# Where the tiles of a one-core encoder block begin in SBUF: small tiles rounded up to 64 bytes

## The chip, the core and the metric

The kernel runs on one core of a Trainium2 chip. The metric is the device time of one execution in microseconds (us), and the median of three executions counts. TensorE (PE in the profile) does the matrix products, VectorE (DVE) and ScalarE (ACT) work on vectors, GpSimd (POOL) and SyncE (SP) mostly issue transfers. SBUF is the on-chip memory from which PE reads both of its operands: the stationary one (the weights, by a LDWEIGHTS instruction, "PEld") and the moving one, which streams through the array in a MATMUL.

## The reference

One layer of an encoder for 256 tokens of width 2048, all in float32:

```
h   = rms_norm(x, norm_g[0])
q, k, v, g, lr, u_f, u_h, u_s = split(h @ w_in)
mix = concat(gla(q, k, v, g, lr), rms_norm(fnet(u_f)),
             rms_norm(hyena(u_h)), rms_norm(shortconv(u_s)))
x   = x + mix @ w_out
x   = x + cross_attention(rms_norm(x, norm_g[1]), rms_norm(mem, mem_norm_g)) # w_xq, w_xkv, w_xo
x   = x + (silu(h3 @ w_gate) * (h3 @ w_up)) @ w_down   # h3 = rms_norm(x, norm_g[2])
return rms_norm(x, final_norm_g)
```

Nearly all of the work is the seven matrices: 4032 blocks of 128x128 weights, each against 256 tokens.

## The kernel before

**Two halves of each number.** To multiply in float32 with fast matmuls, each operand is held as a high part and the rest. A slot of activations is a tile of 128 partitions by 512 columns (2048 bytes in a partition): columns 0 to 255 hold the high part of 256 tokens, columns 256 to 511 the rest. Weights arrive as slabs of 16 blocks (`raw`, 8192 bytes in a partition) by DMA from SP's queue at L79. For each half of a slab ScalarE writes the high part `wh` (L89) and VectorE the rest `wl` (L90). `raw` and `wh`, `wl` rotate through three buffers each, with a fourth pair of `wh`, `wl` until the end of the attention's output product.

**Three ways to multiply by a block.** The method `mm` has two of them. The wide form (L269 and L270) loads `wh` and streams the whole slot, 512 columns, then loads `wl` and streams its first 256 columns. The narrow form (L266, L267 and L270) does three matmuls of 256 columns; it is used in part of the mixers' `w_in` and for the last output tile of `w_down`. The third is `gemm_rows` (L321 to L323): here the activations are stationary, and `wh`, `wl` are the moving operands, 512 columns in each of six matmuls for four blocks. It makes the values of the attention and of the gated linear attention.

**Stages.** In order: keys and values of the memory (`w_xkv`), the mixers (`w_in`), `w_out`, queries and attention (`w_xq`, `w_xo`), the gate and up products (`w_gate_up`), and `w_down`. Between blocks a planner (`Background.poll`) lets generators issue the vector work of earlier results. The order on each engine is fixed when the program is built.

**Slots.** The moving slots are `act0` to `act23` in every stage. In `w_xo`, four of the sixteen are `oex0` to `oex3`. In `w_down`, eight of the 44 are `act` and 36 are `f0` to `f35`. Attention itself streams `kt` (against the stationary `q`, L637 and L638) and `pt` (against `vh`, `vl`, L664 and L665).

**Where the tiles lie.** The pools hand out SBUF in the order in which the tiles are asked for, and each takes its bytes in a partition rounded up to a multiple of 32. The slots `act` and the residuals `res` come first and begin at multiples of 64. Then comes `vec`, 150 columns of float32 or 600 bytes, which takes 608; all that is asked for after it begins 32 bytes past a multiple of 64, until other small tiles shift it back. From the address table of the built program, the start of each tile as a remainder:

| tile | mod 64, before | mod 256, before | mod 64, after | mod 256, after |
|---|---|---|---|---|
| `act`, `res` | 0 | 128 | 0 | 128 |
| `ones`, `ident`, `acc` | 32 | 224 | 0 | 0 |
| `tmp`, `dg` | 32 | 96 | 0 | 192 |
| `raw`, `wh`, `wl` | 32 | 224 | 0 | 0 |
| `f`, `oex`, `pt` | 32 | 224 | 0 | 0 |
| `k2`, `tab`, `gw` and most tiles of the mixers | 32 | 96 | 0 | 128 |
| `kt`, `q`, `vh`, `vl`, `mr` | 0 | 0 | 0 | 64 |

The lines that the change touches are L51 (`NV`, the columns of `vec`), L224 (the columns of scalars of a reciprocal root, `rc` and `krc`), L351 (`warm`), L409 (`sums`), L553 (`qs`) and L645 (the scalars of a softmax).

Of the kernel before, what the change touches and what calls it, by code (L numbers as in the profile page):

```python
# [13 lines left out]
F32 = mybir.dt.float32  # L14
# [8 lines left out]
P = 128  # L23
# [24 lines left out]
V_SCW = 133  # L48
V_B1, V_B2, V_FR = 145, 146, 147
V_NT = 148  # L50
NV = 150  # L51

TWO_PI_1 = 6.28125
TWO_PI_2 = float(np.float32(2 * math.pi - 6.28125))
# [95 lines left out]
class Block:  # L150
# [68 lines left out]
    def rstd_cols(self, p, n, keep=None):  # L219

        nc = self.nc
        m = p.shape[1]
        self.bg.dve(0, 8)
        c = keep.tile([P, 24], F32, name=f"krc{next(self.kept)}") if keep else self.rp.tile([P, 24], F32, name="rc", tag="rc")  # L224
        y, v, a = (c[:, 8 * i:8 * i + m] for i in range(3))
        nc.vector.tensor_scalar(out=v, in0=p, scalar1=1.0 / n, scalar2=EPS, op0=ALU.mult, op1=ALU.add)

        nc.vector.tensor_scalar(out=a.bitcast(U32), in0=v.bitcast(U32), scalar1=1, scalar2=None, op0=ALU.logical_shift_right)
        nc.vector.tensor_scalar(out=y.bitcast(I32), in0=a.bitcast(I32), scalar1=-1.0, scalar2=float(0x5f3759df),
                                op0=ALU.mult, op1=ALU.add)  # L230
        for _ in range(3):
            self.stt(a, y, -0.5, y, ALU.mult, ALU.mult)
            self.tt(a, a, v, ALU.mult)
            self.stt(y, a, 1.5, y, ALU.add, ALU.mult)
        return y
# [95 lines left out]
    def run(self):  # L331
        nc, cp = self.nc, self.cp
        st = self.st
        self.act = [cp.tile([P, 512], F32R, name=f"act{i}") for i in range(24)]
        self.res = [cp.tile([P, 4, R], F32, name=f"res{i}") for i in range(4)]
        self.resk = lambda i: self.res[i // 4][:, i % 4, :]
        self.vec = cp.tile([P, NV], F32, name="vec")
        self.ones = cp.tile([P, P], F32, name="ones")
        self.ident = cp.tile([P, P], F32, name="ident")
        self.acc = cp.tile([P, R], F32, name="acc")  # L340

        self.kd = nc.dram_tensor("keys", (P, 16 * R), F32, kind="Internal").ap()
        self.vd = nc.dram_tensor("values", (P, 8 * 512), F32, kind="Internal").ap()
        nc.scalar.dma_start(self.vec, self.t["vecs"])
        def load(src, k, n):
            nc.sync.dma_start(self.res[k // 4][:, k % 4:k % 4 + n, :].rearrange("p k r -> p (k r)"),
                              self.t[src][:, k * R:(k + n) * R])

        self.load_x = lambda k, n: load("xT", k, n)

        warm = cp.tile([P, 1], F32, name="warm")  # L351
        nc.vector.memset(warm, 1.0)
        nc.scalar.copy(warm, warm)
        load("memT", 0, 1)
        st.after = [lambda: None, lambda: None]
        st.after += [lambda a=a: load("memT", *a) for a in ((1, 1), (2, 1), (3, 1), (4, 1), (5, 1), (6, 2), (8, 2), (10, 2), (12, 2), (14, 2))]
        nc.vector.memset(self.ones, 1.0)
        make_identity(nc, self.ident)
        with self.tc.tile_pool(name="wx", bufs=1) as st.extra:
            self.mixers()  # L360
            self.attention()
        self.mlp()
# [5 lines left out]
    def mixers(self):  # L368
# [37 lines left out]
            nc.vector.tensor_reduce(out=c[:, 0:2], in_=c[:, 2:10].rearrange("p (r k) -> p r k", k=4), axis=AX.X, op=ALU.add)  # L406

        def prepare(mid):
            c = [mid.tile([P, 10], F32, name=f"sums{i}") for i in range(2)]  # L409
            yield 20  # L410
            yield from squares("mem", c[0])
            self.rcm = self.rstd_cols(c[0][:, 0:2], D, self.cp)
            yield
            self.rsm = self.rstd_end(self.rcm, 0, self.cp)
            self.bg.add(hy.filters())
            nc.sync.dma_start(gl.lrw, self.t["lrw"])
            yield from squares("x", c[1])
            col = self.rstd_cols(c[1][:, 0:2], D)
            yield
            self.rsx = self.rstd_end(col, 0, mid)  # L420
# [126 lines left out]
    def attention(self):  # L547
        tc, nc, act, st = self.tc, self.nc, self.act, self.st
        with tc.tile_pool(name="atp", bufs=1) as atp, tc.tile_pool(name="kp", bufs=1) as kp, \
                tc.tile_pool(name="mp", bufs=5) as mp:  # L550
            oex = [atp.tile([P, 512], F32R, name=f"oex{i}") for i in range(4)]
            pt = [atp.tile([P, 512], F32R, name=f"pt{i}") for i in range(2)]
            qs = atp.tile([P, 2], F32, name="qs")  # L553
            o = act[0:8] + oex + act[8:12]
            slot = lambda name, n: kp.tile([P, 512], F32R, name=name, tag=name, bufs=n)
            kv = [([], [], []) for _ in range(4)]

            def ev_q(q, p):
                q.append(slot("q", 8))
                self.split(q[-1], self.merge(p))  # L560

            def scales():

                col = self.rstd_begin([[self.acc]], D)
                nc.vector.tensor_scalar(out=qs, in0=col, scalar1=512 ** -0.5, scalar2=None, op0=ALU.mult)
                yield

            heads = []

            def load_kv():  # L570

                todo = [(hd, what, i) for hd in range(4) for what in range(2) for i in range(4)]
                parts = []

                def fetch():
                    if len(parts) < len(todo):
                        hd, what, i = todo[len(parts)]
                        m = mp.tile([P, R], F32, name="mr", tag="mr")
                        o = (4 * hd + i) * R
                        nc.gpsimd.dma_start(m, (self.vd if what else self.kd)[:, o:o + R])  # L580
                        parts.append(m)

                for _ in range(5):
                    fetch()
                yield 4
                for n, (hd, what, i) in enumerate(todo):
                    while hd > len(heads) + 1:
                        yield
                    if what == 0:
                        kv[hd][0].append(slot("kt", 8))  # L590
                        self.split(kv[hd][0][-1], parts[n])
                    else:
                        if i % 2 == 0:
                            kv[hd][1].append(slot("vh", 4))
                            kv[hd][2].append(slot("vl", 4))
                        c = slice(i % 2 * R, i % 2 * R + R)
                        self.split2(kv[hd][1][-1][:, c], kv[hd][2][-1][:, c], parts[n])
                    fetch()
                    yield 1.0

            def scores(hd, q):
                while len(kv[hd][2]) < 2:
                    yield
                yield
                yield from self.head(q, *kv[hd], pt, o[4 * hd:4 * hd + 4], qs)
                heads.append(hd)

            lp = [list(range(8)), list(range(8, 16))]
            self.bg.add(scales())
            self.bg.add(load_kv())  # L610
            gens = []
            for hd in range(4):
                q = []
                if hd > 1:
                    self.bg.drain(gens[hd - 2], True)
                self.gemm("w_xq", [(4 * hd + i) * P for i in range(4)], self.h2, lambda i, p: ev_q(q, p), first=(4, lp),
                          before=lambda n: n and hd == 0 and self.bg.drain(self.late))
                gens.append(self.bg.add(scores(hd, q)))
            h3 = self.h3 = act[12:24] + act[0:4]

            def ev_o(i, p):
                self.residual(i, p, V_NG + 32 + i, h3[i] if i < 12 else None)
                if i == 12:
                    st.extra = None

            self.gemm("w_xo", [i * P for i in range(16)], o,
                      ev_o,
                      first=(4, [list(range(12)), list(range(12, 16))]), before=lambda n: n == 1 and self.bg.drain())
            self.bg.add(self.rest(h3, 12, V_NG + 32))

    def head(self, q, kt, vh, vl, pt, o, qs):
# [10 lines left out]
        for r in range(2):  # L642
            s = self.merge(ps[r])
            self.tt(s, s, self.rsm, ALU.mult)
            c = self.rp.tile([P, 4], F32, name="rc", tag="sm")  # L645
            nc.vector.tensor_reduce(out=c[:, 0:1], in_=s, axis=AX.X, op=ALU.max)
            self.stt(c[:, 1:2], c[:, 0:1], -1.0, qs[:, r:r + 1], ALU.mult, ALU.mult)
            nc.scalar.activation(s, s, AF.Exp, scale=qs[:, r:r + 1], bias=c[:, 1:2], accum_out=c[:, 2:3])
# [591 lines left out]
```

## Time and profile before

| | us |
|---|---|
| median of three runs | 1525.95 (1525.63 to 1526.79) |
| the profiled execution | 1526.68 |
| its span, first to last instruction | 1524.6 |
| PE busy in the span | 1502.2 |
| DVE busy | 995.5 |
| ACT busy | 787.3 |
| mean granted clock of PE | 0.995 |

The time of the profiled execution is 2.1 us more than its span. A matmul's duration in the profile (394 ns for 512 columns) includes the time in which the next one already streams, since matmuls are pipelined. What a block costs is read from the starts: the time from the start of a matmul to the start of the next.

### The profile page before, as it was taken

Reading aid. Unit: us, or ns where it says so; the run is one execution under the profiler, and the core shown is the slowest. Engines: PE = TensorE matmul, PEld = TensorE weight load, DVE = VectorE, ACT = ScalarE, POOL = GpSimd, SP = SyncE. Lnnn points to the kernel's source line nnn. Section 1 sums busy time; section 2 is a strip of 40 time slices with the busy share of each in tenths; the row PEclk is TensorE's granted clock in tenths of the full one; section 3 lists DMA queues with packets and bytes.
Section 4 is the critical chain, followed back from the end, with each engine's and each line's share of the span. In section 5 each row is a group of like instructions: output and inputs, shape, how many; then the busy total and the mean of one; then the engine's idle time right before and its main releaser. Section 6 shows DMA issues by size and latency. Waiting matters only on the chain.

```text
span 1524.6 us, 22257 instructions
## 1 busy us (share of the span) xinstructions
PE 1502.2 (99%) x8788; PEld 1311.2 (86%) x8788; DVE 995.5 (65%) x1532; ACT 787.3 (52%) x1238; POOL 40.0 (3%) x76
## 2 busy tenths in 40 slices
PE   8999999999999999999999999999999999999996
PEld 7887788889999788888888888888888888888885
DVE  6676668678667766867766666666666664555454
ACT  6664555557445655656554444444444444444442
POOL 0100100000002000100000000000000000000000
PEclk9999999999999999999999999999999999999998
DMA  9965554354346555544545555555555555555552
GB/s 353 343 239 190 198 193 166 139 195 159 139 167 241 195 190 182 177 149 166 194 166 193 189 185 185 189 192 194 193 193 186 186 186 190 192 192 180 183 191 83
DMA packets 48808, 290.53 MB, mean 191 GB/s; under 512 B 6173, under 2 KB 7486, under 8 KB 17088
## 3 DMA queue, kind: packets, MB, share of 16 engines
q1 hardware_dynamic: 44912, 279.59, 51.5%
q0 software_dynamic: 3072, 8.39, 1.6%
q8 instruction: 69, 1.13, 0.3%
q10 hardware_dynamic: 720, 1.13, 0.2%
q14 instruction: 35, 0.29, 0.0%
HBM read 282.80 MB, written 6.29 MB: 190 GB/s over the span
## 4 chain that ended last, share of the span: by engine, by line
PE 96%; DVE 1%; DMA 1%; issue 1%; ACT 0%; SPq 0%; POOL 0%; DVEq 0%; POOLq 0%; ACTq 0%
PE pg L269 49%; PE pg L270 28%; PE pg L266 3%; PE pg L267 3%; PE pg L321 3%; PE pg L323 2%; PE pg L322 2%; PE pm L269 1%; PE pm L796 1%; DMA mr<-values 1%; PE pm L664 1%; PE pm L270 0%; PE pm L637 0%; DMA raw<-in_W 0%; DVE wl L90 0%
## 5 line engine op out<-in xcount | busy, mean ns | idle before, releaser
L269 PE MATMUL pg<-act,wh 128*128 128x512 f32 x2680 | 939.7, 394 | 8.3 <-DVE act L182 4.5
L90 DVE TENSOR_TENSOR wl<-raw,wh 128x1024 fp32r<-128x1024 f32 (+1 forms) x507 | 617.0, 1218 | 425.9 <-ACT wh L89 423.6
L270 PE MATMUL pg<-act,wl 128*128 128x256 f32 x3008 | 842.5, 281 | 0.0
L89 ACT CAST wh<-raw 128x1024 fp32r<-128x1024 f32 (+1 forms) x507 | 529.5, 1046 | 589.5 <-PE pg L269 333.4
L269 PEld LDWEIGHTS pg<-act,wh 128*128 128x128 f32 x2680 | 504.7, 188 | 120.7 <-ACT wh L89 4.5
L270 PEld LDWEIGHTS pg<-act,wl 128*128 128x128 f32 x3008 | 566.9, 189 | 2.6 <-issue 2.0
L269 PE MATMUL pg<-f,wh 128*128 128x512 f32 x540 | 191.3, 398 | 0.0
L270 PE MATMUL pg<-f,wl 128*128 128x256 f32 x576 | 161.8, 281 | 0.0
L269 PEld LDWEIGHTS pg<-f,wh 128*128 128x128 f32 x540 | 101.5, 188 | 25.2
L270 PEld LDWEIGHTS pg<-f,wl 128*128 128x128 f32 x576 | 108.8, 189 | 0.0
L266 PE MATMUL pg<-act,wh 128*128 128x256 f32 x328 | 94.8, 289 | 0.0
L267 PE MATMUL pg<-act,wh 128*128 128x256 f32 x328 | 92.1, 281 | 0.0
L178 DVE TENSOR_TENSOR tmp<-pg,tmp 128x256 f32<-128x256 f32 x183 | 76.2, 417 | 5.7 <-ACT tmp L276 5.0
L276 ACT COPY tmp<-pg 128x256 f32<-128x256 f32 x179 | 65.0, 364 | 14.6 <-PE pg L270 14.5
L321 PE MATMUL pg<-wh,act 128*128 128x512 f32 x160 | 66.4, 415 | 0.0
L323 PE MATMUL pg<-wh,act 128*128 128x512 f32 x160 | 63.3, 395 | 0.0
L322 PE MATMUL pg<-wl,act 128*128 128x512 f32 x160 | 62.9, 393 | 0.0
L266 PEld LDWEIGHTS pg<-act,wh 128*128 128x128 f32 x328 | 61.9, 189 | 0.7
L267 PEld LDWEIGHTS pg<-act,wh 128*128 128x128 f32 x328 | 61.9, 189 | 0.3
L178 DVE TENSOR_TENSOR tmp<-tmp,rs 128x256 f32<-128x256 f32 x88 | 37.3, 425 | 2.9
L321 PEld LDWEIGHTS pg<-wh,act 128*128 128x128 f32 x160 | 30.0, 188 | 10.4 <-issue 2.9
L322 PEld LDWEIGHTS pg<-wl,act 128*128 128x128 f32 x160 | 30.1, 188 | 7.5 <-issue 1.0
(233 smaller groups left out, 985.1 us busy)
## 6 DMA issues: line engine op xcount, KB each, us to landing
raw<-in_W SPq DMA_DIRECT2D x247, 1024.0 KB, 4.8
raw<-in_W SPq DMA_DIRECT2D x9, 512.0 KB, 7.3
res<-in_xT SPq DMA_DIRECT2D x8, 512.0 KB, 5.6
k<-in_mem SPq DMA_DIRECT2D x8, 256.0 KB, 9.0
k<-in_x SPq DMA_DIRECT2D x8, 256.0 KB, 8.2
keys<-tmp POOLq DMA_DIRECT2D x16, 128.0 KB, 5.7
values<-tmp POOLq DMA_DIRECT2D x16, 128.0 KB, 2.4
mr<-keys POOLq DMA_DIRECT2D x16, 128.0 KB, 3.5
```

The source lines that it names most:

```text
L89: nc.scalar.copy(wh[:, a:b], r[:, a:b])
L90: nc.vector.tensor_tensor(out=wl[:, a:b], in0=r[:, a:b], in1=wh[:, a:b].bitcast(F32), op=ALU.subtract)
L178: self.nc.vector.tensor_tensor(out=out, in0=a, in1=b, op=op)
L266: self.nc.tensor.matmul(p[:, 0:R], wh, slot[:, 0:R], start=start, stop=False)
L267: self.nc.tensor.matmul(p[:, 0:R], wh, slot[:, R:512], start=False, stop=False)
L269: self.nc.tensor.matmul(p[:, :], wh, slot[:, :], start=start, stop=False)
L270: self.nc.tensor.matmul(p[:, 0:R], wl, slot[:, 0:R], start=False, stop=stop)
L276: self.nc.scalar.copy(t, p[:, R:512])
L321: nc.tensor.matmul(ps[r][:, :], hi, wh, start=k == 0, stop=False)
L322: nc.tensor.matmul(ps[r][:, :], hi, wl, start=False, stop=False)
L323: nc.tensor.matmul(ps[r][:, :], lo, wh, start=False, stop=k == nk - 1)
L664: nc.tensor.matmul(p[:, :], vh[m][:, s], pt[m][:, :], start=m == 0, stop=False)
```

## The change

Six small tiles are made a multiple of 64 bytes: `vec` has 160 columns in place of 150 (640 bytes), the scalars of a reciprocal root 32 in place of 24 (128 bytes), the softmax's scalars 16 in place of 4, `sums` 16 in place of 10, and `warm` and `qs` take 16 columns, of which the first one and the first two are used. The host fills the ten new columns of `vec` with zeros. Every tile of 256 bytes or more then begins at a multiple of 64 (table above). The instructions of each engine and their order are the same in both programs, but for the DMA of `vec` (L344), which brings 128x160 numbers in place of 128x150.

```diff
-NV = 150
+NV = 160
...
-        c = keep.tile([P, 24], F32, name=f"krc{next(self.kept)}") if keep else self.rp.tile([P, 24], F32, name="rc", tag="rc")
+        c = keep.tile([P, 32], F32, name=f"krc{next(self.kept)}") if keep else self.rp.tile([P, 32], F32, name="rc", tag="rc")
...
-        warm = cp.tile([P, 1], F32, name="warm")
+        warm = cp.tile([P, 16], F32, name="warm")[:, 0:1]
...
-            c = [mid.tile([P, 10], F32, name=f"sums{i}") for i in range(2)]
+            c = [mid.tile([P, 16], F32, name=f"sums{i}") for i in range(2)]
...
-            qs = atp.tile([P, 2], F32, name="qs")
+            qs = atp.tile([P, 16], F32, name="qs")[:, 0:2]
...
-            c = self.rp.tile([P, 4], F32, name="rc", tag="sm")
+            c = self.rp.tile([P, 16], F32, name="rc", tag="sm")
```

## The prediction

> **What bounds the kernel now.** I read the page first, then the chain of waits, then the starts of the matmuls in the timeline.
>
> ```profile
> span 1524.6 us, 22257 instructions
> ...
> PE 1502.2 (99%) x8788; PEld 1311.2 (86%) x8788; DVE 995.5 (65%) x1532; ACT 787.3 (52%) x1238; POOL 40.0 (3%) x76
> ...
> PE 96%; DVE 1%; DMA 1%; issue 1%; ACT 0%; SPq 0%; POOL 0%; DVEq 0%; POOLq 0%; ACTq 0%
> ```
>
> PE sets the end: 96% of the chain is its matmuls. The program after has the same instructions in the same order, so the change can move the time only if an instruction's speed depends on where its tiles begin. The trace holds that comparison already, because some moving operands begin at a multiple of 64 bytes (`act`, `kt`) and others 32 past one (`f`, `oex`, `pt`, and `wh`, `wl` in `gemm_rows`). The groups by line and form in the stage of `w_down` (window 1285 to 1480 us; count, then busy us and mean ns):
>
> ```profile
> L269 PE MATMUL pg<-f,wh 128*128 128x512 f32 x454 | 160.8, 398 | 0.0
> L270 PE MATMUL pg<-f,wl 128*128 128x256 f32 x454 | 127.5, 281 | 0.0
> L269 PE MATMUL pg<-act,wh 128*128 128x512 f32 x101 | 35.6, 392 | 0.0
> L270 PE MATMUL pg<-act,wl 128*128 128x256 f32 x101 | 28.2, 280 | 0.0
> ```
>
> Same stage, same weight buffers, same shapes, no idle: 512 columns from `f` take 6 ns more than from `act`. The starts say what a block costs. Timelines of PE (start us, duration us); two from `w_down`, one from the attention, one from `gemm_rows`:
>
> ```profile
> 1319.67 0.40 PE L269 MATMUL pg<-f,wh 128*128 128x512 f32 x1
> ...
> 1323.55 0.39 PE L269 MATMUL pg<-act,wh 128*128 128x512 f32 x1
> ```
>
> ```profile
> 1304.17 0.39 PE L269 MATMUL pg<-act,wh 128*128 128x512 f32 x1
> ...
> 1306.60 0.40 PE L269 MATMUL pg<-f,wh 128*128 128x512 f32 x1
> ```
>
> ```profile
> 600.39 0.39 PE L637 MATMUL pm<-kt,q 128*128 128x512 f32 x1
> ...
> 602.12 0.39 PE L637 MATMUL pm<-kt,q 128*128 128x512 f32 x1
> ```
>
> ```profile
> 104.28 0.39 PE L323 MATMUL pg<-wh,act 128*128 128x512 f32 x1
> ...
> 106.38 0.39 PE L323 MATMUL pg<-wh,act 128*128 128x512 f32 x1
> ```
>
> Between the first two lines lie 11 blocks of `f`: 3.88/11 = 353 ns each. In the second pair, 7 blocks of `act`: 2.43/7 = 347. In the third, 5 blocks of `kt` against `q`, where both operands begin at a multiple of 64: 1.73/5 = 346. In the last, 9 matmuls of 512 columns with `wh`, `wl` moving: 2.10/9 = 233.3. Over all blocks of the trace, from the start of one to the start of the next, with those more than 15% over the median (waits) left out: `act` 346.9 ns (2636 blocks, nearly all 346 or 347), `f` 353.0 (539, in a cycle of 349, 350, 361), `oex` 351.4 (63), `pt` 352.4 (29). In the narrow form, three matmuls of 256 columns take 355.4 from `act` and 360.0 from `f`.
>
> The cycle of `f` is 1060 ns for three blocks, that of `act` 1040: 6.67 ns a block. A wide block and a narrow matmul give the pace of one column: 355.4/3 = 118.5 ns for 256 columns and 346.9 - 118.5 = 228.4 for 512, so 109.9/256 = 0.43 ns. So the difference is some 15.5 columns, or 62 bytes of a partition: it reads as one 64-byte piece more to fetch, where a run of columns begins inside such a piece. That is my reading; the sum needs only the rows.
>
> **The change, part by part.** Each moving operand that now begins at 32 past a multiple of 64 will cost what one on a multiple costs.
>
> 1. `f`, wide: 540 blocks x (353.0 - 346.9) = 3.3 us; by the steady cycles, 540 x 6.67 = 3.6.
> 2. `f`, narrow (the last output tile): 36 blocks x (360.0 - 355.4) = 0.2 us.
> 3. `oex`: 64 x (351.4 - 346.9) = 0.3; `pt`: 32 x (352.4 - 346.9) = 0.2.
> 4. `gemm_rows`: L321, L322 and L323 come 160 times each, so 480 matmuls. No row shows 512 columns on a multiple of 64 followed by another 512; the nearest is the 228.4 worked out above. 480 x (233.3 - 228.4) = 2.4 us. Bounds: 480 x 6.67 = 3.2 at most; nothing, if the 233.3 belongs to 512 columns behind 512. I take 2.4, since 4.9 ns is close to what `f` shows.
>
> Sum 3.3 + 0.2 + 0.5 + 2.4 = 6.4 us off the path, as nothing else waits there: in the windows 99 to 204 us and 1262 to 1497 us PE is busy 105.00 of 105 and 235.00 of 235, and in the latter DVE 119.6 and ACT 106.6. Weights keep up: ACT's L89 idles 333.4 us of the span until PE frees a `wh`, that is, the buffers are full and PE is late, not ACT. If that cover were gone, PE would wait at L269 for `wh`; a shortening by 1.7% doesn't reach it.
>
> Edits that I cost at nothing:
>
> - *The blocks on `act`* (2680 and 64 wide, 328 narrow): the moving tile stays where it is, `wh` and `wl` under it move from 32 to 0 mod 64. The nearest row is `kt` with `q`, both on multiples: 346 against 347. Bounds: a gain of 0.4 ns x some 3300 wide blocks = 1.3 us; the loss is the last rival.
> - *ScalarE and VectorE.* Casts `kt<-mr` (all on multiples) took 405 ns, `act<-tmp` (source 32 past) 406; the subtractions 419 and 419. They lie beside PE except from 464 to 498 us, where the chain runs over ACT, DVE and the loads of `mr`, and in the 14 us after the last matmul: 2 ns in 405 over 48 us is 0.2 us either way.
> - *DMAs.* `vec` brings 40 bytes more in a partition, 5 KB, at the 353 GB/s of the first slice 0.01 us; ACT waited 0.70 us for it, but the chain runs over a `raw` that lands later (a piece of 5.07 us from 2.14). `raw` itself now lands on multiples of 64; ACT's L89 waited 5.4 us for it in all, so that and no more could go. I take 0, and 0.3 for the range.
>
> A page speaks against all of this: the Trainium skill, "SBUF — State Buffer", section "Specifications", gives lines of 16 bytes in SBUF and a penalty for each access that crosses to a new one. By it a tile at 32 past a multiple of 64 begins on a line as well as any other, and the sum would be zero, 1525.95 us; the 353 against 347 ns here disagree with it.
>
> The profiled execution took 1526.68 us (span 1524.6); 1526.7 - 6.4 = 1520.3. It lies 0.7 above the median of the three runs, so for the median 1525.95 - 6.4 = **1519.6 us**. Own range of this case: 1525.95 - (3.6 + 0.2 + 0.4 + 0.2 + 3.2 + 1.3 + 0.3) = 1516.8, and 1521 where items 3 and 4 come out at half.
>
> **The rivals.**
>
> - *The rows keep their price.* 512 columns behind 512 might cost 233 wherever they begin. For it: L322 follows L321 on the same stationary tile, which no wide block does. Against: the extra is that of `f`. Then 1525.95 - 4.0 = 1522.0.
> - *No change.* The price of `f` may come from something that stays: `f` and `wh` have the same remainder mod 256 before (224) and after (0), `act` and `wh` have different ones. If equal remainders of moving and stationary tile are what costs, `f`, `oex` and `pt` against the weights stay as they are, and the rows too: 1525.95. Against it: `kt` and `q` are equal mod 256 and run at 346; in `gemm_rows` the two differ and it is slow. The 16-byte lines of the page above end in this case too.
> - *Slower.* The same mechanism with remainders mod 64: before, `act` (0) differs from `wh` (32), and after it the two are equal in every block on `act`, as `f` and `wh` are now. Then 2744 wide blocks x 6.1 = 16.7 us and 328 narrow x 4.6 = 1.5 come on top and nothing is won: 1544 us. It is slower by more than can be told from no change once 17% of these blocks pay (3.05 of 18.2). Only `kt` with `q` speaks against it directly, 30 blocks; their mean is 350.3, since groups begin with a slower one, but the steady ones are at 346 to 347.
> - That the change doesn't do what it says is excluded by the address table.
>
> **How the numbers follow.** Forecast 0.70, rows keep their price 0.13, no change 0.12, slower 0.05. A measurement can tell about 0.2%, 3.05 us, from no change: both of the first two are faster by more (6.4 and 4.0). So faster 0.83, same 0.12, slower 0.05. The first two hold 0.83, so the range need reach no further: from 1516.8 to the 1522.0 of the second and 1.4 more, 1523.4, for the spread of the runs (0.8 from the median to the highest) and for item 3 coming out at nothing (0.5).
>
> **What would show it.** In the profile after: `f` blocks at 347 in place of 353 in `w_down`, L269 on `f` at 392 in place of 398; nine matmuls of `gemm_rows` in 2.06 us in place of 2.10; `act` blocks still at 347; durations of L89 and L90 as before. The `w_down` stage shorter by 3 to 4 us, the rest of the gain where `gemm_rows` runs, 99 to 204 us and a second time shortly before 332. Wrong would be `f` still in its cycle of 349, 350, 361, or `act` blocks in it.

## The result, and the profile after

The kernel after takes 1536.84 us (median of six runs, 1534.88 to 1538.39) against 1525.79 for the kernel before (1524.66 to 1527.40): a ratio of 1.0071, 95% interval 1.0059 to 1.0084. It is slower by 11.05 us, where 6.4 us less were forecast. The profiled execution took 1534.88 us.

The page of the kernel after, the lines that answer to the first fence of the prediction:

```profile
span 1532.8 us, 22257 instructions
...
PE 1511.0 (99%) x8788; PEld 1316.5 (86%) x8788; DVE 995.5 (65%) x1532; ACT 787.3 (51%) x1238; POOL 39.9 (3%) x76
...
PE 96%; DVE 1%; DMA 1%; issue 0%; ACT 0%; SPq 0%; POOL 0%; DVEq 0%; POOLq 0%; ACTq 0%
```

PE alone has grown, by 8.8 us busy (its weight loads by 5.3); VectorE and ScalarE are where they were to the tenth. The groups by line and form in `w_down` of the kernel after (window 1295 to 1490 us; count, then busy us and mean ns):

```profile
L269 PE MATMUL pg<-f,wh 128*128 128x512 f32 x450 | 159.6, 399 | 0.0
L270 PE MATMUL pg<-f,wl 128*128 128x256 f32 x449 | 126.1, 281 | 0.0
L269 PE MATMUL pg<-act,wh 128*128 128x512 f32 x104 | 37.0, 393 | 0.0
L270 PE MATMUL pg<-act,wl 128*128 128x256 f32 x104 | 29.4, 283 | 0.0
```

`f` now begins at a multiple of 64 and has won nothing: 399 ns, before 398. `act`, which has not moved, has lost: 393 and 283 in place of 392 and 280. The starts say it more plainly. First 15 blocks of `act` in `w_gate_up` of the kernel before, then 15 of the kernel after, from the timelines of PE (start us, duration us):

```profile
999.85 0.39 PE L269 MATMUL pg<-act,wh 128*128 128x512 f32 x1
...
1005.05 0.39 PE L269 MATMUL pg<-act,wh 128*128 128x512 f32 x1
```

```profile
999.79 0.39 PE L269 MATMUL pg<-act,wh 128*128 128x512 f32 x1
...
1005.05 0.39 PE L269 MATMUL pg<-act,wh 128*128 128x512 f32 x1
```

5.20/15 = 347 ns a block before, 5.26/15 = 351 after. Over the whole trace, with blocks more than 15% over the median left out as in the prediction:

| from start to start, ns | before | after | count |
|---|---|---|---|
| wide block on `act` | 346.9 | 351.0 | 2744 |
| wide block on `f` | 353.0 | 353.4 | 540 |
| wide block on `oex` | 351.4 | 350.4 | 64 |
| narrow block on `act` | 355.4 | 355.9 | 328 |
| narrow block on `f` | 360.0 | 359.8 | 36 |
| three matmuls of `gemm_rows` | 700.2 | 697.2 | 160 |

The sum is 2744 x 4.1 + 540 x 0.4 - 64 x 1.0 + 328 x 0.5 - 36 x 0.2 - 160 x 3.0 = 11.1 us: the 11.05 of the medians. The two profiled executions differ by 8.2 only; most of the gap is accounted for in the last section.

### The profile page after: what moved, and what is told of

It is laid out like the page before. It is cut to its first block, busy times and chain, and to the rows that moved or that the text cites. A ratio compares the mean times of both kernels' runs of the same rounds, so it can differ in the third digit from the quotient of the medians.

```text
span 1532.8 us, 22257 instructions
## 1 busy us (share of the span) xinstructions
PE 1511.0 (99%) x8788; PEld 1316.5 (86%) x8788; DVE 995.5 (65%) x1532; ACT 787.3 (51%) x1238; POOL 39.9 (3%) x76
## 4 chain that ended last, share of the span: by engine, by line
PE 96%; DVE 1%; DMA 1%; issue 0%; ACT 0%; SPq 0%; POOL 0%; DVEq 0%; POOLq 0%; ACTq 0%
PE pg L269 49%; PE pg L270 28%; PE pg L266 3%; PE pg L267 3%; PE pg L321 3%; PE pg L323 2%; PE pg L322 2%; PE pm L269 1%; PE pm L796 1%; DMA mr<-values 1%; PE pm L270 1%; PE pm L664 1%; PE pm L637 0%; DMA raw<-in_W 0%; DVE wl L90 0%
## 5 line engine op out<-in xcount | busy, mean ns | idle before, releaser
L269 PE MATMUL pg<-act,wh 128*128 128x512 f32 x2680 | 948.1, 395 | 7.8 <-DVE act L182 4.6
L89 ACT CAST wh<-raw 128x1024 fp32r<-128x1024 f32 (+1 forms) x507 | 528.9, 1044 | 595.8 <-PE pg L269 336.8
L269 PEld LDWEIGHTS pg<-act,wh 128*128 128x128 f32 x2680 | 504.0, 188 | 124.4 <-ACT wh L89 4.6
L269 PE MATMUL pg<-f,wh 128*128 128x512 f32 x540 | 191.5, 399 | 0.0
L269 PEld LDWEIGHTS pg<-f,wh 128*128 128x128 f32 x540 | 101.5, 188 | 25.1
```

What stands on the lines that cost most here:

```text
L89: nc.scalar.copy(wh[:, a:b], r[:, a:b])
L269: self.nc.tensor.matmul(p[:, :], wh, slot[:, :], start=start, stop=False)
```

## The experiments

Throughout, the *distance* is the start of the weights (`wh`, and `wl`, which has the same remainder unless said) less the start of the moving slot, mod 256. In the kernel before it is 96 on `act` (224 - 128) and 0 on `f` (224 - 224); after, 128 on `act` and still 0 on `f`. In every experiment the instructions and their order are those of the kernel before or after; only unused tiles are added, or a size is changed.

**32 bytes alone.** The kernel before with one unused tile of 32 bytes, so that `wh` and all behind it shift by 32 and `vec` and the other small tiles keep their sizes.

```diff
         self.acc = cp.tile([P, R], F32, name="acc")
+        cp.tile([P, 8], F32, name="pad")
```

> The kernel before, with one unused tile of 32 bytes behind acc, so that all that is asked for after it moves up by 32 bytes and nothing else differs (vec keeps its 150 columns). wh, wl, raw, f, oex and pt go from 32 to 0 mod 64, as in the kernel after; act stays at 0. Theory A (what costs is that the moving slot and the weights have equal starts mod 64): act blocks at 351 ns in place of 346.9, f blocks at 353 as before, 1537 us. Theory B (the starts do not matter; the wider vec or another of the small tiles does it): act blocks at 347, 1526 us. Theory C (the exact distance matters, not its remainder mod 64): anything between.

Measured 1537.42 us against 1527.13, ratio 1.0067 (1.0052 to 1.0082). `act` at 351.0 ns, `f` at 353.4, as in the kernel after. So the sizes of the small tiles and the wider `vec` cost nothing that shows: the shift alone gives the whole loss.

**64 bytes.** The same with 16 columns in place of 8.

> The kernel before with an unused tile of 64 bytes behind acc: wh, wl, raw, f, oex, pt stay at 32 mod 64, but go from 224 to 32 mod 256. Theory A: as before, act blocks 347 ns, 1526 us. Theory C with remainders mod 256: act blocks at another pitch than 347, by up to 6 ns either way, 1526 plus or minus up to 16 us.

1535.50 us, ratio 1.0053 (1.0038 to 1.0068). `wh` is at 32 mod 64 again, and `act` at 0, as in the kernel before, yet `act` runs at 350.6 ns (350.0 in `w_gate_up`): theory A, that equal remainders mod 64 are slow and different ones fast, fell here. The distance is 160. Two blocks of `act` 15 apart in `w_gate_up`:

```profile
999.80 0.39 PE L269 MATMUL pg<-act,wh 128*128 128x512 f32 x1
...
1005.05 0.39 PE L269 MATMUL pg<-act,wh 128*128 128x512 f32 x1
```

5.25/15 = 350 ns. And `f`, still at distance 0, ran at 347.0; more of that below.

**`f` moved by 32 bytes.** Only `f`, so that its distance goes from 0 to 224.

```diff
+            fp.tile([P, 8], F32, name="pad")
             f = act[4:12] + [fp.tile([P, 512], F32R, name=f"f{i}") for i in range(36)]
```

> The kernel before with an unused tile of 32 bytes ahead of f0 only: the f slots begin at 0 mod 64, wh and wl stay at 32, as act and wh stand now. Theory A: f blocks go from 353 to 347 ns, 540 x 6.1 = 3.3 us less, 1522.5 us, all other blocks as before. Theory D (the weights' own start sets the price, whatever moves): f blocks stay at 353, 1526 us.

1523.64 us, ratio 0.9973 (0.9964 to 0.9983). `f` at 346.7 ns, narrow `f` at 350.1 in place of 360.0, all else as before. So the blocks on `f` could be had for less, as the prediction had it; but by moving `f` against its weights, not by moving both.

**`act` moved instead.** The kernel after with 32 bytes ahead of `act0`, and `vec` cut by 32 bytes, so that every tile behind `vec` lies where it lies in the kernel after: only `act`, `res` and the small tiles next to them have moved.

```diff
-NV = 160
+NV = 152
...
+        cp.tile([P, 8], F32, name="pad")
         self.act = [cp.tile([P, 512], F32R, name=f"act{i}") for i in range(24)]
```

> The kernel after with 32 unused bytes ahead of act0 and vec at 152 columns in place of 160: act and res begin at 32 mod 64, every later tile lies exactly where it lies in the kernel after (wh, f at 0 mod 256). The distance of act to wh is then 96 mod 256, as in the kernel before. Theory A: act blocks back at 347 ns, f blocks at 353, about 1526 us. Theory D (the weights' own start on a multiple of 64 is what is slow): act blocks stay at 351, 1537 us.

1526.73 us, ratio 0.9996 (0.9987 to 1.0006). `act` is back at 346.9 ns, against weights that begin at a multiple of 256. Again two blocks 15 apart:

```profile
999.84 0.39 PE L269 MATMUL pg<-act,wh 128*128 128x512 f32 x1
...
1005.04 0.39 PE L269 MATMUL pg<-act,wh 128*128 128x512 f32 x1
```

5.20/15 = 347 ns. What costs is neither operand's own start but their distance: 96 here and before.

**All eight distances.** Two kernels, each run once: the kernel before with pads between the slots; the slots of `f` stand in four groups of nine at four distances each.

```diff
+            f = act[4:12]
+            for i in range(36):
+                n = {9: 8, 18: 8, 27: 8}.get(i) # the second kernel: {0: 32, 9: 8, 18: 8, 27: 8}
+                if n:
+                    fp.tile([P, n], F32, name=f"fpad{i}")
+                f.append(fp.tile([P, 512], F32R, name=f"f{i}"))
```

> The kernel before with small unused tiles between the slots, so that one run shows several distances of the start of wh (and wl) to that of the moving slot, mod 256: in w_down f0 to f8 0, f9 to f17 224, f18 to f26 192, f27 to f35 160; in w_gate_up and earlier act0 to act11 96 as before, act12 to act15 64, act16 to act19 32, act20 to act23 0. wh stays at 224 mod 256. Read from the start-to-start time of each block. Theory A (equal mod 64 is slow, 32 apart is fast): f 353, 347, 353, 347 ns; act 347, 353, 347, 353. Theory E (the distance mod 128 decides, 96 fast, the rest slow): f 353, 347, slow, slow; act12 to act23 all slow at 350 to 353. Theory F (the price hangs on the cycle that the stream was in before, not on the distance): the groups run on in whatever pitch they are entered with.

> The same with the other distances mod 256: f0 to f8 128, f9 to f17 96, f18 to f26 64, f27 to f35 32; act12 to act15 224, act16 to act19 192, act20 to act23 160, act0 to act11 96. Theory A: f 353, 347, 353, 347 ns; act12 to act23 347, 353, 347. Theory E: f 353, 347, slow, 350; act12 to act23 347, slow, 350. Theory F: pitches run on across the groups.

One column of `w_down` of the first sweep, timeline of PE: the start of the third and of the ninth block at distance 0, then two blocks six apart at 224, at 192 and at 160.

```profile
1347.92 0.40 PE L269 MATMUL pg<-f,wh 128*128 128x512 f32 x1
...
1350.04 0.40 PE L269 MATMUL pg<-f,wh 128*128 128x512 f32 x1
...
1351.10 0.39 PE L269 MATMUL pg<-f,wh 128*128 128x512 f32 x1
...
1353.18 0.39 PE L269 MATMUL pg<-f,wh 128*128 128x512 f32 x1
...
1354.56 0.40 PE L269 MATMUL pg<-f,wh 128*128 128x512 f32 x1
...
1356.68 0.40 PE L269 MATMUL pg<-f,wh 128*128 128x512 f32 x1
...
1357.39 0.40 PE L269 MATMUL pg<-f,wh 128*128 128x512 f32 x1
...
1359.49 0.39 PE L269 MATMUL pg<-f,wh 128*128 128x512 f32 x1
```

Six blocks take 2.12, 2.08, 2.12 and 2.10 us: 353, 347, 353 and 350 ns. The pitch changes within three blocks of each border, so here it belongs to the distance and does not run on across the groups as theory F had it. One column of the second sweep, two blocks six apart at distance 96 and at 64:

```profile
1363.85 0.39 PE L269 MATMUL pg<-f,wh 128*128 128x512 f32 x1
...
1365.93 0.39 PE L269 MATMUL pg<-f,wh 128*128 128x512 f32 x1
...
1366.97 0.39 PE L269 MATMUL pg<-f,wh 128*128 128x512 f32 x1
...
1369.09 0.40 PE L269 MATMUL pg<-f,wh 128*128 128x512 f32 x1
```

2.08/6 = 347 and 2.12/6 = 353. On `f` in these two kernels (and on `act` at 96 and at 128 before and after) each distance falls into a cycle of its own, in every column:

| distance mod 256 | cycle, ns | a block |
|---|---|---|
| 96, 224 | 346, 347, 347 | 346.7 |
| 160 | 349, 351 | 350 |
| 128 | 346, 354, 353 or 346, 354, 354 | 351 |
| 0 | 349, 350, 361 | 353.3 |
| 192 | 349, 356, 355 | 353.3 |
| 64 | 353, 354, 353 | 353.3 |
| 32 | 346, 361 | 353.5 |

Two of eight are fast. Theory E, with remainders mod 128, gives too few classes: 0 and 128 differ, and so do 32 and 160. A layout in which all large tiles begin at multiples of 64 has only the distances 0, 64, 128 and 192 to choose from, and none of these is fast in this table; but 0 and 192 have a second, lower pitch in other runs (below). The order is that of the wide form: narrow blocks on `act` took 351 ns at 192 as at 224, 355 at 96 and 356 at 128. The slots of `act` in the two sweeps, four to a group in `w_gate_up`, agree where they can be read: 347 at 224 and 349, 351 at 160; at the other distances four blocks are too few for a cycle to settle. (The single times, 1531.15 and 1528.33 us beside 1529.2, mix good and bad groups and say nothing more.)

**The whole layout moved by 64.** The kernel before with 64 bytes ahead of `act0`: all distances stay.

> The kernel before with 64 unused bytes ahead of act0: every tile moves up by 64 and all distances stay; wh, wl, f lie at 32 mod 256, as in e2_pad64, where f blocks took 347 ns at distance 0. Theory E (the distance of the start of the weights to that of the moving slot, mod 256, sets the pitch: 96 and 224 fast at 347, 0, 32, 64 and 192 at 353, 128 at 351, 160 at 350): 1526 us, act blocks at 347. For f, which is at distance 0: if the place itself counts, 347 as in e2_pad64 and 1522.5 us; if the cycle in which the stream enters f counts (act at 347 here and before, at 350 in e2_pad64), 353 and 1526 us.

1527.17 us, ratio 1.0003 (0.9994 to 1.0013); `act` at 346.9 ns, `f` at 353.0. `wh`, `wl` and `f` lie at the very addresses that they have in the run with 64 bytes behind `acc`, where `f` took 347. So distance 0 has two pitches, and the addresses of these tiles do not choose between them. What differs is the stream on `act` ahead of `f`, at distance 160 there and at 96 here; that its cycle chooses is the natural reading, and not shown.

**The kernel after, and 64 bytes more.** All large tiles still begin at multiples of 64; `act` goes to distance 192.

> The kernel after with an unused tile of 64 bytes behind acc: all large tiles still begin at multiples of 64, act is at distance 192 in place of 128. Theory E: act blocks 353.4 in place of 351.0, 2744 x 2.4 = 6.6 us more than the kernel after, some 1543 us, ratio to before 1.011; f blocks at 353 as before. Theory A (multiples of 64 are all alike): act blocks 351, 1537 us.

1539.05 us, ratio 1.0081 (1.0067 to 1.0096). `act` in `w_gate_up` runs at 353.3 ns, in the cycle of the table, so multiples of 64 are not alike: 128 gave 351. The 1543 us of the expectation were too high: narrow blocks fell to 351.3, and over all stages `act` is at 352.8, since at the same distance it ran at 349 in some stretches (721 to 780 us). This run also shows both pitches of distance 0 side by side. From its timeline, two columns of `w_down`, the same slots of `f` both times:

```profile
1284.11 0.40 PE L269 MATMUL pg<-f,wh 128*128 128x512 f32 x1
...
1289.06 0.40 PE L269 MATMUL pg<-f,wh 128*128 128x512 f32 x1
...
1293.27 0.39 PE L269 MATMUL pg<-f,wh 128*128 128x512 f32 x1
...
1297.78 0.39 PE L269 MATMUL pg<-f,wh 128*128 128x512 f32 x1
```

The first column makes 14 blocks in 4.95 us (354 ns), the next 13 in 4.51 (347). Ahead of both, `act` runs in the same cycle of 348, 357, 355 and leaves it at a different one of the three; so the distance of the stream ahead does not decide by itself either.

**Fast distances for `f` and `oex`, then for all.** The kernel before with 32 bytes ahead of `oex0` and of `f0`; then, besides, 128 bytes behind `acc`, which puts `act` at 224 too.

```diff
         self.acc = cp.tile([P, R], F32, name="acc")
+        cp.tile([P, 32], F32, name="pad") # in the second kernel alone
...
+            atp.tile([P, 8], F32, name="pad")
             oex = [atp.tile([P, 512], F32R, name=f"oex{i}") for i in range(4)]
...
+            fp.tile([P, 8], F32, name="pad")
             f = act[4:12] + [fp.tile([P, 512], F32R, name=f"f{i}") for i in range(36)]
```

> The kernel before with 32 unused bytes ahead of oex0 and ahead of f0: f and oex go from distance 0 to 224, all else as before. Theory E: f blocks 346.7 (3.3 us less), narrow f blocks 350 in place of 360 (0.4), oex blocks 347 in place of 351 (0.3): 4.0 us less, ratio 0.9974.

> The same with 128 unused bytes more behind acc, so that act too is at distance 224 in place of 96. Theory E: wide blocks at 347 as before, f at 346.7; narrow act blocks at 350 in place of 355, as narrow f at 224 in e3_f32, 328 x 5 = 1.7 us less; 5.5 us less than before in all, ratio 0.9964. A theory in which 224 was fast only for f: act blocks leave 347 and it is slower by up to 16 us. gemm_rows, whose distances change too, may add or take 1 us.

1523.23 us, ratio 0.9977 (0.9967 to 0.9987), and 1522.13 us, ratio 0.9969 (0.9957 to 0.9981). In the second, `act`, `oex` and `f` all run at 346.7 to 346.9 ns, narrow `act` at 351.1 in place of 355.4, narrow `f` at 350.1. Both beat both kernels; between the two the intervals overlap.

**Which load pays.** Pads between the buffers of `wh` and `wl`. In the first kernel `act` has `wh` at 96 and `wl` at 192, in the second `wh` at 192 and `wl` at 96.

```diff
         wh = pool.tile([P, 1024], F32R, name="wh", tag="wh")
+        pool.tile([P, 24 if pool is self.extra else 8], F32, name="wpad", tag="wpad") # x3 in the ring
         wl = pool.tile([P, 1024], F32R, name="wl", tag="wl")
```

> The kernel before with unused tiles of 96 bytes in all between the buffers of wh and those of wl: on act blocks wh stays at distance 96 (fast) and wl goes to 192 (slow when both are there, 353 in e8_after64). On f wh is at 0 and wl at 96. If the load of wl pays, which runs beside the 512 columns of wh's matmul: act blocks at 353 ns and about 1542 us, f at 347. If the load of wh pays, which runs beside the 256 columns of wl's matmul: act at 347 and f at 353, 1526 us. If each pays half or the two together make the cycle: act between, 350, some 1535 us.

> The mirror image: on act blocks wh at distance 192 and wl at 96; on f wh at 0 and wl at 160. If the load of wl pays: act at 347 and about 1526 us. If the load of wh pays: act at 353 and about 1542 us. If each pays: act at 350, some 1535 us.

1528.38 us, ratio 1.0012 (0.9999 to 1.0026), and 1526.90 us, 0.9999 (0.9990 to 1.0009). In `w_gate_up` `act` runs at 348.3 and 348.9 ns, some 2 ns over 346.7, where both loads at 192 gave 353.3. But in the first kernel the same blocks, at the same two distances, ran at 353.3 from 205 to 603 us. Two pairs of blocks 12 apart, one from each stretch (here L272 is L269 of the kernel before):

```profile
540.15 0.40 PE L272 MATMUL pg<-act,wh 128*128 128x512 f32 x1
...
544.39 0.40 PE L272 MATMUL pg<-act,wh 128*128 128x512 f32 x1
```

```profile
1000.06 0.40 PE L272 MATMUL pg<-act,wh 128*128 128x512 f32 x1
...
1004.24 0.40 PE L272 MATMUL pg<-act,wh 128*128 128x512 f32 x1
```

4.24/12 = 353 and 4.18/12 = 348 ns. So this pair of distances has two pitches too, and which load pays stays open. In these two kernels, moving one load off 96 was enough to raise the pitch, whichever load it was. Two of the ten runs of the first kernel took 1534.44 and 1535.68 us at a granted clock no lower than that of the others (0.995 and 0.996): the 1408 blocks of `w_gate_up` at 353.3 in place of 348.3 would be 7.0 us more than the median, an estimate that fits, but there is no trace of these runs. The medians are lower than the 1535 that was expected, since `f`, with its two distances also apart now, went from 353.0 to 347.1 and 347.2 (3.1 us less), and `gemm_rows` fell from 700.2 to 693.8 and 695.6 (1.0 and 0.7 us).

## Why the prediction was wrong

**The step that failed** is the one before the list: "Each moving operand that now begins at 32 past a multiple of 64 will cost what one on a multiple costs." The comparison that it rests on was sound: `f` took 353 and `act` 347 in the same stage, with the same weight buffers and no wait. But the two differ in two ways, in their own start and in their distance to the weights, and the change moves `f` and the weights together. It kept the distance that cost (0 on `f`) and spoilt the one that did not (96 on `act`, to 128).

Item by item. Items 1 and 2, `f`: 3.5 us forecast, a loss of 0.2 measured. Item 3, `oex` and `pt`: 0.5 forecast, 0.1 measured. Item 4, `gemm_rows`: 2.4 forecast, 0.5 measured (697.2 for three). The 62 bytes that were worked out of the cycles, and their reading as one more 64-byte piece, do not hold: in the kernel after, `act` begins on a multiple of 64 and runs at 351 ns; in the same kernel with `act` moved it begins 32 past one and runs at 347.

*The blocks on `act`* were costed at nothing, with `kt` against `q` as the nearest row, and they are the whole loss: 2744 x 4.1 = 11.3 us. That row was a poor witness. `kt` and `q` are at distance 0, which has two pitches. In the kernel before, the first two heads settled at 346 and 347, and the last one went through 349, 350, 361; the steady stretch that I quoted was the good one. The last head, two blocks six apart (2.12/6 = 353 ns):

```profile
680.48 0.40 PE L637 MATMUL pm<-kt,q 128*128 128x512 f32 x1
...
682.60 0.40 PE L637 MATMUL pm<-kt,q 128*128 128x512 f32 x1
```

The mean of 350.3 over all 30 blocks, which I had put down to slow beginnings, already said so.

**The rivals.** "Slower" had the right kind of cause, the relation between the two operands, and the right place, the blocks on `act`; it got 0.05. Its price of 16.7 us had the wrong size, as `act` went to a cycle of 351 and not of 353, and its rule, equal remainders mod 64, is refuted by the run with 64 bytes. "No change" had seen that `f` and `wh` keep the same remainder, and on `f` the price did stay. Put together, the two rivals describe the result; kept apart, each could be argued against with `kt` and with `gemm_rows`.

What held: nothing but PE moved; ScalarE and VectorE were as busy as before to the tenth, and ScalarE's L89 waited 4.1 us for `raw` in place of 5.4; the gap of 6 ns on `f` could be closed (3.5 us of 1527).

The lines of the Trainium skill that were weighed ("SBUF — State Buffer", "Specifications": lines of 16 bytes) would have given no change. The runs disagree with that as they do with the forecast: shifts by 32 bytes, two such lines, make a block 347 or 353 ns. The same page, in "A bandwidth-pool intuition that's wrong (but worth ruling out)", gives PE a second, independent read port for the weight loads. By it the distance should not matter; the pitches by distance say that in this kernel the time of load and stream together hangs on where the two lie. That the load of the next weights and the stream of the slot get in each other's way is the natural reading, but no run shows the conflict itself, and the last two experiments do not tell which load it would be. Why 96 and 224 are free, what sets the length of the cycles, and what chooses between two pitches at one distance, stays open.

## What to carry to other kernels

In a kernel bound by back-to-back fp32 matmuls, look at the start-to-start time of matmuls by stage: a steady cycle that differs between two tiles of the same shape can be a matter of addresses. Compare the *distance* between stationary and moving tile, not the alignment of either. Pads of 32 to 128 bytes that changed it moved this kernel's time by 0.2 to 0.7%, in either direction; 64 bytes ahead of everything, which kept it, moved nothing that shows. An edit that only resizes a small tile early in a pool can do the same by accident. When one row of a trace is to carry an argument, check that it is steady over all its occurrences.

## What the runs showed of the hardware besides

**A half clock after a stall, by chance.** At the start of the attention PE waits 3 to 5 us in every trace for VectorE and the loads of `mr`. During that wait, or at its end, the granted clock fell to half for 6.8 us in the profile of before and in three of the experiments, for 3.4 in eight others, and not at all in one more and in that of after. Windows just behind the wait, before and after (us, then busy us and number of instructions of each engine, granted clock, share of DMA, GB/s):

```profile
499.00:506.00 7.00, 7.00 (x26) 6.01 (x27) 6.77 (x14) 5.23 (x12) 1.64 (x3) 0.61 0.76 242
```

```profile
501.00:508.00 7.00, 7.00 (x41) 6.14 (x41) 6.93 (x14) 5.23 (x12) 1.63 (x3) 1.00 0.79 259
```

26 matmuls in 7 us against 41. Of the 6.8 us PE was busy for 5.5, so half a clock cost 2.7 us of work: with these the difference of the two profiled executions, 8.2 us, becomes 10.9, beside 11.05 for the medians. It can be a part of the spread of the runs of one kernel (1 to 5 us, and 9 in the one named above); the runs that were not profiled show only a mean clock of 0.994 to 0.997. The Trainium skill, "TensorE: Matmul & The Clock Gate", "Part 1: The HAM clock gate", has free-running windows of some 3.4 us after which an idle PE falls to half its clock; the 0, 3.4 and 6.8 us here agree in length. The waits do not sort them: one of 2.75 us, shorter than such a window, was followed by half a clock, and those of 3.16 (after) and 3.22 us were not.

**Two pitches at one distance.** At distance 0 the same slots against the same rotating weight buffers run at 347 or at 353 ns for a whole column, and at distance 192 `act` runs at 349 or at 353. Within a steady stretch the pitch holds until other slots or a wait come between. At 96, 224, 128 and 160 these traces show one steady pitch of the wide blocks each.
